# Chunked RWKV-7 in a hybrid trunk: three inverses in turn on half banks, packed squares, sliced products

## The chip, the cores and the metric

One core of a Trainium2 chip runs the whole program in one launch. The metric is device time in microseconds, the median of several executions. TensorE (PE in the views, PEld its weight loads) does matmuls and transposes, VectorE (DVE) and ScalarE (ACT) work on tiles and copy out of PSUM, GpSimd (POOL) does some products in SBUF, and SyncE (SP) issues most DMAs.

## The reference

One inference step of a decoder trunk of two layers, all in float32: 512 prompt tokens behind 16 meta tokens, and 8 sample rows of one token each, which share the weights. The kernel keeps all of them as T = 536 columns (528 of the prompt, TP, and 8 of the samples).

```
for each layer:
  x += 1/2 SwiGLU_a(RMSNorm(x));  x += Mixer(RMSNorm(x));  x += 1/2 SwiGLU_b(RMSNorm(x))
even mixer: HGRN2 (4 heads of 128) beside RWKV-7 (8 heads of 64), one output projection
odd mixer:  GLA (4 heads, keys 128, values 256)
RWKV-7, per head and token:
  S_t = S_{t-1} diag(w_t) + (S_{t-1} (-kk_t)) (kk_t * a_t)^T + v_t k_t^T;   y_t = S_t r_t
HGRN2, GLA: S_t = diag(f_t) S_{t-1} + k_t v_t^T;   o_t = S_t^T q_t
RWKV-7 output: group norm of y per head, plus a bonus term, times a gate; HGRN2 output: RMSNorm
```

The states of the samples come in as inputs and leave as outputs; the prompt starts from zero.

## The kernel before, in words

Activations are held with channels on the 128 partitions and tokens along the free axis. Each large projection is a run of **dense** matmuls (L240 to L242 and L334 to L336): operands are split into a high and a low part (`hh`, `hl`, `whi`, `wlo`) and three products are summed in a PSUM bank of tag `d`.

**RWKV-7 on the prompt** is computed in chunks (`CHUNKS`, one of 16 tokens and eight of 64), for two head pairs at a time: group d = 0 or 1 holds the pairs 2d and 2d+1, so there are 18 chunk problems. `waves(pool, R)` (L1121) writes them as steps. `stage_g` lays four rows of a chunk (keys, values and the two of the update) out in the block tile `bd` (row layout, L1155), multiplies them against each other (L1159 to L1161) and transposes them (L1170). Then the inverse of a triangular matrix is built by doubling: `lev_t` (product L1182, from level 2 a transpose L1187, copies by ScalarE L1188 and L1190) and `lev_x` (L1204, a masked copy by VectorE L1206), over five levels (three for the chunk of 16). When an inverse is done, five steps use it: `st_p` (L1215 to L1224), `st_t`, `st_sa` (L1236), `st_s` (state, L1251) and `st_y` (L1261, L1264). A table `slots` sets the order of all 280 steps: the two groups run side by side, the second `LAG` places behind, and the five output steps of a chunk stand among the next chunk's levels, a place each.

**PSUM.** There are eight banks of 2 KB per partition. `psum(d=2, m=2, w=4)` gives the waves two banks for dense work, two for the HGRN2 core and the sample rows (`m`) and four for `waves` (`w`); `bank(tag)` hands out the next one of a tag's ring.

**The order on TensorE** is written by hand in `even_mixer` (the block under `tc.manual_schedule`): its instructions are issued there in the order in which the generators emit them. The loop takes one step of `waves`, then fills. Every `SAMPLE_EVERY`-th step it takes one piece of `ts`, the sample rows of RWKV-7 (`rsample`, L1060, four pairs one after the other: transposes, a round through DRAM, then products on GpSimd and sums on VectorE, with the tiles `acc` and `sq` that exist once each). Every `POST_EVERY`-th step it takes a piece of `po`, the group norm and gate (`rpost`, L1304) of one span of tokens out of `SPANS`; `post()` starts only when the HGRN2 projections of the fourth head exist (`3 not in H`), and `hgrn_norm` comes before it once the HGRN2 cores are done. `hgrn_norm` sums squares in `acc` and `sq`, and `rpost` uses the same two tiles. After each step the loop adds `FILL` to a credit (in columns of dense work) and spends it on `th_`: the projections and cores of HGRN2 (`hproj`, `hcore`), then the first half of the output projection (`mix_out`). What is left of `th_`, `po` and `mo` follows after the last step. The HGRN2 core of one head (`gla_core`) goes over eight levels of scores (L627, L638 on TensorE; decayed keys L658 on GpSimd); `gla_step` beside it does the sample rows, with the output product of the states at L736. The odd mixer uses the same two functions.

```
credit = min(credit + FILL, FILL_MAX)
while credit > 0:
    cost = next(th_, None)
```

Outside the even mixer (FFNs, odd mixer) nothing of this order is touched, save the output product of `gla_step`.

## Time and profile before

| What | Value |
|---|---|
| Runs, us | 2305.34, 2306.35, 2305.53 (median 2305.53) |
| The execution profiled, us | 2313.27 (span 2311.5) |
| TensorE busy | 2256.8 us, 98% |
| Its weight loads | 2206.5 us, 95% |
| VectorE busy | 1646.7 us, 71% |
| ScalarE busy | 1082.8 us, 47% |
| GpSimd busy | 143.5 us, 6% |
| TensorE clock granted, mean | 0.991 |

The even mixer's waves take from about 516 us to 868 us of the span. A float32 matmul of the non-dense kind has two records in the trace, so that a group with x280 is 140 matmuls. The share of busy time is an average over stages with different limits; what a change is worth in a stage is read from the waits and durations there. Of TensorE's clock the column PEclk gives the part of full speed that was granted: 1.00 is 2.4 GHz, 0.50 is 1.2 GHz.

### The profile page before, as it was taken

Reading aid. Unit: us, or ns where it says so; the run is one execution under the profiler, and the core shown is the slowest. Engines: PE = TensorE matmul, PEld = TensorE weight load, DVE = VectorE, ACT = ScalarE, POOL = GpSimd, SP = SyncE. Lnnn points to the kernel's source line nnn. Section 1 sums busy time; section 2 is a strip of 40 time slices with the busy share of each in tenths; the row PEclk is TensorE's granted clock in tenths of the full one; section 3 lists DMA queues with packets and bytes.
Section 4 is the critical chain, followed back from the end, with each engine's and each line's share of the span. In section 5 each row is a group of like instructions: output and inputs, shape, how many; then the busy total and the mean of one; then the engine's idle time right before and its main releaser. Section 6 shows DMA issues by size and latency. Waiting matters only on the chain.

```text
span 2311.5 us, 47443 instructions
## 1 busy us (share of the span) xinstructions
PE 2256.8 (98%) x19520; PEld 2206.5 (95%) x19520; DVE 1646.7 (71%) x2971; ACT 1082.8 (47%) x2056; POOL 143.5 (6%) x192
## 2 busy tenths in 40 slices
PE   8999999999999999999999999999999999999998
PEld 8999999998998888999999999999999889999998
DVE  7858576686666878966757885857666777948576
ACT  6525254374444456434535452525434464525355
POOL 0000000312212100000000000000021210000000
PEclk9999999999999999999999999999999999999999
DMA  6323334223222116242423332333434353333324
GB/s 171 106 78 101 92 92 132 81 64 94 79 71 72 49 49 167 74 119 75 118 74 101 92 110 74 101 92 94 128 110 128 111 160 92 92 92 101 110 85 136
DMA packets 409393, 229.23 MB, mean 99 GB/s; under 512 B 19252, under 2 KB 400501, under 8 KB 409176
## 3 DMA queue, kind: packets, MB, share of 16 engines
q1 hardware_dynamic: 408456, 224.78, 33.5%
q8 instruction: 153, 2.51, 0.5%
q10 hardware_dynamic: 720, 1.42, 0.2%
q14 instruction: 64, 0.52, 0.1%
HBM read 211.19 MB, written 14.97 MB: 98 GB/s over the span
## 4 chain that ended last, share of the span: by engine, by line
PE 86%; DVE 5%; DMA 3%; ACT 2%; issue 1%; POOL 1%; SPq 0%; ACTq 0%; POOLq 0%; DVEq 0%
PE d L334 21%; PE d L335 21%; PE d L336 21%; PE d L240 5%; PE d L242 4%; PE d L241 4%; PE w L1182 1%; PE w L1204 1%; DMA vb<-dv 1%; DVE wlo L229 1%; DMA raw<-in_even_w_out_dram 1%; PE m L155 1%; DMA sq<-dr 1%; DMA raw<-in_odd_w_out_dram 1%; PE w L1187 1%
## 5 line engine op out<-in xcount | busy, mean ns | idle before, releaser
L240 PE MATMUL d<-hh,whi 128*128 128x264 f32 (+2 forms) x1136 | 343.6, 303 | 2.0 <-DVE xT L596 1.3
L242 PE MATMUL d<-hh,wlo 128*128 128x264 f32 (+2 forms) x1136 | 326.7, 288 | 1.9 <-DVE wlo L229 1.7
L241 PE MATMUL d<-hl,whi 128*128 128x264 f32 (+2 forms) x1136 | 326.6, 288 | 0.5 <-DVE hl L1418 0.5
L334 PE MATMUL d<-hh,whi 128*128 128x268 f32 (+1 forms) x832 | 237.8, 286 | 1.8 <-ACT hh L187 1.3
L335 PE MATMUL d<-hl,whi 128*128 128x268 f32 (+1 forms) x832 | 238.1, 286 | 0.9 <-DVE hl L188 0.9
L336 PE MATMUL d<-hh,wlo 128*128 128x268 f32 (+1 forms) x832 | 237.7, 286 | 0.7 <-DVE wlo L293 0.7
L240 PEld LDWEIGHTS d<-hh,whi 128*128 128x128 f32 x1136 | 216.1, 190 | 7.5 <-issue 2.4
L242 PEld LDWEIGHTS d<-hh,wlo 128*128 128x128 f32 x1136 | 215.4, 190 | 4.6 <-DVE wlo L229 4.0
L241 PEld LDWEIGHTS d<-hl,whi 128*128 128x128 f32 x1136 | 216.3, 190 | 0.9 <-DVE hl L1418 0.7
L534 DVE SCALAR_TENSOR_TENSOR xT<-d,xT 128x272 f32<-128x272 f32 (+2 forms) x192 | 82.9, 433 | 166.7 <-PE d L336 166.6
L334 PE MATMUL d<-hid,whi 128*128 128x264 f32 (+2 forms) x704 | 201.5, 287 | 0.0
L334 PE MATMUL d<-hid,whix 128*128 128x264 f32 (+2 forms) x704 | 201.2, 286 | 0.0
L335 PE MATMUL d<-hid,whix 128*128 128x264 f32 (+2 forms) x704 | 200.8, 285 | 0.0
L335 PE MATMUL d<-hid,whi 128*128 128x264 f32 (+2 forms) x704 | 200.7, 286 | 0.0
L336 PE MATMUL d<-hid,wlox 128*128 128x264 f32 (+2 forms) x704 | 200.6, 285 | 0.0
L336 PE MATMUL d<-hid,wlo 128*128 128x264 f32 (+2 forms) x704 | 200.5, 286 | 0.0
L334 PE MATMUL d<-sumh,whix 128*128 128x268 f32 (+1 forms) x576 | 170.9, 297 | 0.0
L336 PE MATMUL d<-sumh,wlo 128*128 128x268 f32 (+1 forms) x576 | 164.7, 286 | 0.0
L335 PE MATMUL d<-suml,whix 128*128 128x268 f32 (+1 forms) x576 | 164.4, 285 | 0.0
L334 PE MATMUL d<-sumh,whi 128*128 128x268 f32 (+1 forms) x576 | 164.2, 285 | 0.0
L336 PE MATMUL d<-sumh,wlox 128*128 128x268 f32 (+1 forms) x576 | 164.0, 285 | 0.0
L335 PE MATMUL d<-suml,whi 128*128 128x268 f32 (+1 forms) x576 | 164.0, 285 | 0.0
(383 smaller groups left out, 6557.8 us busy)
## 6 DMA issues: line engine op xcount, KB each, us to landing
raw<-in_ffn_gate_dram SPq DMA_DIRECT2D x44, 512.0 KB
raw<-in_ffn_up_dram SPq DMA_DIRECT2D x44, 512.0 KB
rawx<-in_ffn_gate_dram SPq DMA_DIRECT2D x44, 512.0 KB
rawx<-in_ffn_up_dram SPq DMA_DIRECT2D x44, 512.0 KB
raw<-in_ffn_down_dram SPq DMA_DIRECT2D x32, 512.0 KB
rawx<-in_ffn_down_dram SPq DMA_DIRECT2D x32, 512.0 KB
raw<-in_even_w_in_dram SPq DMA_DIRECT2D x30, 512.0 KB
raw<-in_odd_w_in_dram SPq DMA_DIRECT2D x25, 512.0 KB
```

Source lines behind the costliest of these rows:

```text
L155: nc.tensor.matmul(ps[:, :b - a], lhsT, rhs[:, a:b], start=True, stop=True)
L229: nc.vector.tensor_sub(lo[:, ks], raw[:, ks], hi[:, ks].bitcast(F32))
L240: nc.tensor.matmul(o, hi[:, k], h, start=(k == 0), stop=False)
L241: nc.tensor.matmul(o, hi[:, k], l, start=False, stop=False)
L242: nc.tensor.matmul(o, lo[:, k], h, start=False, stop=(k == nk - 1))
L334: nc.tensor.matmul(o, hi[:, k], rh(k), start=start and k == 0, stop=False, **kw)
L335: nc.tensor.matmul(o, hi[:, k], rl(k), start=False, stop=False, **kw)
L336: nc.tensor.matmul(o, lo[:, k], rh(k), start=False, stop=stop and k == nk - 1, **kw)
L534: nc.vector.scalar_tensor_tensor(xv[:, sl], ps, -0.5, xv[:, sl], ALU.mult, ALU.add)
L1182: nc.tensor.matmul(pt[rs, 128 * i:128 * i + cs.stop], U["gm"][ks, i, rs], U["xx"][ks, i, cs], start=True, stop=True)
L1187: nc.tensor.transpose(px[:, 128 * i:128 * i + 128], U["xx"][:, i, 0:128], ident)
L1204: nc.tensor.matmul(pd[:, i], lhsT, rhs, start=True, stop=True)
```

## The change

It changes the order of the waves and the size of several of their products:

- **Three inverses side by side** (`CHAINS`) instead of two. The 18 chunk problems alternate between the groups and take the next free of three chains; a chain's steps stand `CHAINS` places apart, the chains start `STAGGER` apart, and the five output steps stand `OUT_STEP` places apart.
- **Half banks.** `bank("w")` hands out the two halves of one bank one after the other; the first stage takes two halves for its products, and one product of level 0 for both pairs shares a half.
- **Packed squares.** The products L1182 and L1204 of all levels but the last keep only the 32-column blocks on the diagonal: four matmuls with 32 columns of the left operand in the place of one with 128 (`squares_mm`); the result of a pair is 32 columns wide, and `into` spreads it under the mask. The level-0 product is cut in the same way.
- **Row layout copies** (`bd`) are made by ScalarE instead of VectorE.
- **Slices.** The output product of the sample states in `gla_step` is cut into four slices of 32 columns, that of `st_y` into two of 64.
- **Fill.** `FILL` is 550 instead of 1100, `SAMPLE_EVERY` 6 instead of 3, `POST_EVERY` 5 instead of 3, and the first span of `SPANS` is cut in two.

The diff, cut to its core:

```diff
-FILL, FILL_MAX = 1100, 5000
+FILL, FILL_MAX = 550, 5000
...
-SAMPLE_EVERY, POST_EVERY = 3, 3
-SPANS = [0, 272, 400, 536]
-LAG, LAG_LATER = 2, 3
+SAMPLE_EVERY, POST_EVERY = 6, 5
+SPANS = [0, 144, 272, 400, 536]
+CHAINS, STAGGER, OUT_STEP = 3, 4, 2
...
     def bank(tag="m"):
-        return til(rings[tag][0], [P, 512], tag)
+        if tag != "w":
+            return til(rings[tag][0], [P, 512], tag)
+        if not halves:
+            t = til(rings[tag][0], [P, 512], tag)
+            halves.extend((t[:, 256:512], t[:, 0:256]))
+        return halves.pop()
...
-                    nc.tensor.matmul(po[:, c:c + 1], st[:, b, 128 * i:128 * i + 128],
-                                     q[:, TP + b0 + b:TP + b0 + b + 1], start=True, stop=True)
+                    for r in range(0, P, 32):
+                        nc.tensor.matmul(po[r:r + 32, c:c + 1], st[:, b, 128 * i + r:128 * i + r + 32],
+                                         q[:, TP + b0 + b:TP + b0 + b + 1], start=True, stop=True)
...
-                    nc.vector.tensor_copy(dst, Q["sl"][hs, 0:4, t0:t0 + n].rearrange("p v (a l) -> p v a l", l=nl))
-                g = bank("w")
+                    nc.scalar.copy(dst, Q["sl"][hs, 0:4, t0:t0 + n].rearrange("p v (a l) -> p v a l", l=nl))
+                g, gl = bank("w"), bank("w")
...
-                nc.tensor.matmul(g[:, 0:128], b_[:, 384:512], b_[:, 0:128], start=True, stop=True)
+                lt = gl if i == 0 else lt
+                for a in range(na):
+                    for h in range(2):
+                        q = 64 * a + 32 * h
+                        nc.tensor.matmul(lt[q:q + 32, 32 * i:32 * i + nl], b_[:, 384 + q:416 + q],
+                                         Q["sl"][:, 0, t0 + 32 * a:t0 + 32 * a + nl], start=True, stop=True)
...
-                nc.vector.copy_predicated(U["xx"][:, i, 0:128], cu[:, CU_R:CU_R + 128], g[:, 0:128])
...
+                nc.tensor.transpose(gl[:, 128:256], b_[:, 0:128], ident)
                 pt = bank("w")
-                for v in range(3):
-                    nc.tensor.transpose(pt[:, 128 * v:128 * v + 128], b_[:, 128 * v:128 * v + 128], ident)
-                nc.scalar.copy(U["tm"][:, i], pt[:, :384])
+                for v in range(2):
+                    nc.tensor.transpose(pt[:, 128 * v:128 * v + 128], b_[:, 128 * v + 128:128 * v + 256], ident)
+                nc.scalar.copy(U["tm"][:, i, 0:128], gl[:, 128:256])
+                nc.scalar.copy(U["tm"][:, i, 128:384], pt)
+            into(U, 0, lt, 64 * na, nl)
...
+        def into(U, li, ps, rows, nl):
+            src = ps[:rows, 0:64].rearrange("p (u c) -> p u c", u=2)[:, :, :nl]
+            mk = cu[:rows, CU_R + 256 * li:CU_R + 256 * li + 128].rearrange("p (b c) -> p b c", b=4)
+            xx = U["xx"][:rows, :, 0:128].rearrange("p u (b c) -> p u b c", b=4)
+            nc.vector.copy_predicated(xx[:, :, :, :nl], mk.unsqueeze(1).to_broadcast([rows, 2, 4, 32])[:, :, :, :nl],
+                                      src.unsqueeze(2).to_broadcast([rows, 2, 4, nl]))
+        def squares_mm(ps, lhs, rhs):
+            for i in range(2):
+                for q in range(0, P, 32):
+                    nc.tensor.matmul(ps[q:q + 32, 32 * i:32 * i + 32], lhs[:, i, q:q + 32], rhs(i, q),
+                                     start=True, stop=True)
...
+            else:
+                U["t1"] = til(pool, [P, 2, 32], "t1c", bufs=CHAINS)
+                squares_mm(pt, U["gm"], lambda i, q: U["xx"][:, i, q:q + 32])
...
+            if not last:
+                squares_mm(ps, xx[:, :, 128:256], lambda i, q: t1[:, i])
+                into(U, li, ps, P, 32)
+                return
...
-                nc.tensor.matmul(py[:, 64 * i:64 * i + n], U["sa"][:, i], U["gm"][:, i, 128:128 + n],
-                                 start=True, stop=True)
+                for r in (slice(0, 64), slice(64, 128)):
+                    nc.tensor.matmul(py[r, 64 * i:64 * i + n], U["sa"][:, i, r], U["gm"][:, i, 128:128 + n],
+                                     start=True, stop=True)
...
+        free = [STAGGER * i for i in range(CHAINS)]
+        after, ends = [0, 0], []
+        for c in range(18):
+            d, w, U = c % 2, c // 2, {}
+            k = free.index(min(free))
+            t = max(free[k], ends[c - CHAINS - 1] if c > CHAINS else 0)
+            for fn in inverse(d, w, U):
+                slots.setdefault(t, []).append((1 + k, fn, 0))
+                t += CHAINS
+            free[k] = t
+            t = max(t - CHAINS + 2, after[d])
+            for i, st in enumerate((st_p, st_t, st_sa, st_s, st_y)):
+                fn = lambda st=st, d=d, w=w, U=U: st(d, w, U)
+                slots.setdefault(t + OUT_STEP * i, []).append((0, fn, int(i == 4)))
+            after[d] = t + 4 * OUT_STEP
+            ends.append(after[d])
```

In the order of the whole program TensorE's instructions go from 17633 to 18889: the 136 matmuls each of L1182 and L1204 that are not of the last level become 544 each with 32 columns, the 36 of L1159 become 136, and the 96 of L736 become 384. The 280 steps of the waves stay 280. Between the first and the last inverse there are 351 dense matmuls where there were 579.

How the order moves is shown at three places. First TensorE in a first stage, before (`bd` is the row layout of a pair, `sl` the rows themselves, `cf` the identity; the number behind `w` is the PSUM tile's):

```order
L1159 MATMUL w_9717<-bd_820_6034 128x128
L1160 MATMUL w_9717<-sl_613_4515,bd_820_6034 128x128
L1161 MATMUL w_9717<-sl_613_4515,bd_820_6034 128x128
L1170 MATMUL w_9724<-cf_66,bd_820_6034 128x128 x3
L1159 MATMUL w_9731<-bd_821_6036 128x128
L1160 MATMUL w_9731<-sl_616_4518,bd_821_6036 128x128
L1161 MATMUL w_9731<-sl_616_4518,bd_821_6036 128x128
L1170 MATMUL w_9738<-cf_66,bd_821_6036 128x128 x3
```

Here products and transposes take tiles w_9717, w_9724, w_9731 and w_9738, a bank each. Now, with the semaphores that an instruction waits on (DVE, Activation and PE stand for VectorE, ScalarE and TensorE itself):

```order
L1175 MATMUL w_8114<-sl_607_4509,bd_820_6034 32x32 [waits PE_49]
L1175 MATMUL w_8114<-sl_607_4509,bd_820_6034 32x32 x3
L1177 MATMUL w_8114<-sl_607_4509,bd_820_6034 128x128
L1178 MATMUL w_8114<-sl_607_4509,bd_820_6034 128x128
L1184 MATMUL w_8114<-cf_66,bd_820_6034 128x128 [waits DVE_49]
L1187 MATMUL w_8124<-cf_66,bd_820_6034 128x128 [waits PE_49]
L1187 MATMUL w_8124<-cf_66,bd_820_6034 128x128
L1175 MATMUL w_8114<-sl_610_4512,bd_821_6036 32x32 [waits Activation_49]
L1175 MATMUL w_8114<-sl_610_4512,bd_821_6036 32x32 x3
L1177 MATMUL w_8124<-sl_610_4512,bd_821_6036 128x128 [waits Activation_49]
L1178 MATMUL w_8124<-sl_610_4512,bd_821_6036 128x128
```

The transpose of the first pair goes into w_8114, the tile of its products, and waits for VectorE; the second pair's products go into w_8114 and w_8124, which the first pair used, and wait for ScalarE.

Second, TensorE around the transposes of the fourth pair's sample rows (L1069 before, L1081 now), before (`d` is dense work, `hh` and `hl` its left, `whi` and `wlo` its right operands):

```order
L1236 MATMUL w_8471<-pp_8419,xx_7878 128x128 x2
L240 MATMUL d_8318<-hh_70,whi_8311 128x272
L241 MATMUL d_8318<-hl_71,whi_8311 128x272
L242 MATMUL d_8318<-hh_70,wlo_8312 128x272
L1204 MATMUL w_8479<-t_1333_8425,xx_8375 128x128 x2
L1069 MATMUL m_8484<-cf_66,sl_616_4518 8x128
L1069 MATMUL m_8484<-cf_66,ws_618_4520 8x128
L1069 MATMUL m_8484<-cf_66,sl_616_4518 8x128 x2
L1069 MATMUL m_8493<-cf_66,sl_616_4518 8x128
L240 MATMUL d_8318<-hh_70,whi_8311 128x272
```

They stand among the levels of the inverses, with dense matmuls before and behind. Now (L723 and L724 are the outputs of the fourth HGRN2 core; L166 into `m` is the sum of squares of `hgrn_norm` from `acc`, L166 into `w` the group norm of `rpost`):

```order
L723 MATMUL m_11098<-acc_10813,vt_11065 128x128
L724 MATMUL m_11098<-hq_10197,S_11090 128x128
L1081 MATMUL m_11115<-cf_66,sl_616_4518 8x128
L1081 MATMUL m_11115<-cf_66,ws_618_4520 8x128
L1081 MATMUL m_11115<-cf_66,sl_616_4518 8x128 x2
L1081 MATMUL m_11124<-cf_66,sl_616_4518 8x128
L166 MATMUL m_11169<-acc_11157,cf_66 128x272
L166 MATMUL m_11173<-acc_11157,cf_66 128x264
L166 MATMUL w_11190<-sl_607_4509,cf_66 128x144
L166 MATMUL w_11190<-sl_610_4512,cf_66 128x144
L166 MATMUL w_11197<-acc_11189,cf_66 128x144
```

They stand behind the last wave and behind the fourth head's core, and the sum of `hgrn_norm` and the group norm of the first span follow with nothing between.

Third, GpSimd at the same place, before (L1091 to L1115 are the products of the sample rows, L658 the decayed keys of an HGRN2 core):

```order
L658 TENSOR_TENSOR hk_7598<-hk_7598,dlev_8267 128x16x16
L1091 TENSOR_TENSOR sq_8566<-acc_8564,sq_8566 128x512
L658 TENSOR_TENSOR hk_7598<-hk_7598,dlev_8267 128x8x32
L1098 TENSOR_TENSOR acc_8564<-acc_8564,sq_8738 128x512
L658 TENSOR_TENSOR hk_7598<-hk_7598,dlev_8267 128x4x64
L1102 TENSOR_TENSOR sq_8832<-sq_8832,ws_618_4520 128x512
L1103 TENSOR_TENSOR acc_8564<-acc_8564,sq_8832 128x512
L1108 TENSOR_TENSOR sq_8905<-sq_8905,sl_616_4518 128x512
L1109 TENSOR_TENSOR acc_8564<-acc_8564,sq_8905 128x512
L1115 TENSOR_TENSOR sq_9040<-acc_8564,sq_9040 128x512
```

The sample products of the last pair run among the key products of the third head. Now (L669 are the key products, L1103 to L1127 the sample products):

```order
L669 TENSOR_TENSOR hk_10558<-hk_10558,dlev_10816 128x16x16
L669 TENSOR_TENSOR hk_10558<-hk_10558,dlev_10816 128x8x32
L669 TENSOR_TENSOR hk_10558<-hk_10558,dlev_10816 128x4x64
L1103 TENSOR_TENSOR sq_11132<-acc_11130,sq_11132 128x512
L1110 TENSOR_TENSOR acc_11130<-acc_11130,sq_11137 128x512
L1114 TENSOR_TENSOR sq_11141<-sq_11141,ws_618_4520 128x512
L1115 TENSOR_TENSOR acc_11130<-acc_11130,sq_11141 128x512
L1120 TENSOR_TENSOR sq_11146<-sq_11146,sl_616_4518 128x512
L1121 TENSOR_TENSOR acc_11130<-acc_11130,sq_11146 128x512
L1127 TENSOR_TENSOR sq_11152<-acc_11130,sq_11152 128x512
```

They come behind the last key product of the fourth head, with nothing of the even mixer behind them.

## Rows read from the trace of the kernel before

**Rows 1.** The page, busy time of each engine (us, share of the span, records).

```profile
PE 2256.8 (98%) x19520; PEld 2206.5 (95%) x19520; DVE 1646.7 (71%) x2971; ACT 1082.8 (47%) x2056; POOL 143.5 (6%) x192
```

**Rows 2.** Windows: length, busy us and records of PE, PEld, DVE, ACT, POOL; PEclk, DMA share, GB/s.

```profile
516.00:868.00 352.00, 332.73 (x3439) 311.02 (x3437) 247.34 (x713) 163.29 (x441) 71.45 (x78) 0.98 0.24 69
```

**Rows 3.** Groups by line and form on PE: busy us, mean ns of one record.

```profile
L1182 PE MATMUL w<-xx,gm 128*128 128x128 f32 x280 | 45.0, 284 | 1.9 <-DVE xx L1206 1.9
L1204 PE MATMUL w<-t,xx 128*128 128x128 f32 x272 | 43.2, 283 | 1.3 <-ACT xx L1190 0.6 <-ACT t L1188 0.5
L736 PE MATMUL m<-hq,st 128*128 128x1 f32 x192 | 25.9, 239 | 2.1 <-DVE acc L621 1.2 <-ACT whi L228 0.8
```

**Rows 4.** Timeline of one level step in the waves: start us, us, engine, line, operation.

```profile
776.49 0.61 PE L1182 MATMUL w<-xx,gm 128*128 128x128 f32 x4
776.93 0.38 PE L1187 MATMUL w<-cf,xx 128*128 128x128 f32 x2
777.18 0.37 ACT L1188 COPY t<-w 128x256 f32<-128x256 f32 x1 [0.44 <-PE w L1182]
777.45 0.38 ACT L1190 COPY xx<-w 128x256 f32<-128x256 f32 x1
```

**Rows 5.** Timeline of PE in the odd mixer, runs of 32-column operands and one-column products.

```profile
1692.52 0.46 PE L627 MATMUL m<-hq,hk 128*32 128x32 f32 x32
1692.90 0.39 PE L240 MATMUL d<-hh,whi 128*128 128x256 f32 x1
1693.13 0.28 PE L241 MATMUL d<-hl,whi 128*128 128x256 f32 x1
...
1850.92 0.50 PE L736 MATMUL m<-hq,st 128*128 128x1 f32 x4
1851.36 0.46 PE L627 MATMUL m<-hq,hk 128*32 128x32 f32 x32
```

**Rows 6.** Timeline of a first stage in the waves.

```profile
820.59 0.49 PE L1170 MATMUL w<-cf,bd 128*128 128x128 f32 x3
...
821.12 0.48 ACT L1171 COPY tm<-w 128x384 f32<-128x384 f32 x1
...
821.19 0.35 DVE L1166 TENSOR_TENSOR gm<-w,cf 128x192 f32<-128x192 f32 x1
```

**Rows 7.** The same timeline, two copies out of one bank by two engines.

```profile
820.12 0.26 ACT L1222 COPY pd<-w 64x128 f32<-64x128 f32 x1
...
820.41 0.29 DVE L1222 COPY pd<-w 64x128 f32<-64x128 f32 x1 [1.00 <-ACT pd L1222]
```

**Rows 8.** Timeline of one pair's sample step: its first transpose, last product, last sum.

```profile
642.85 0.27 PE L1069 MATMUL m<-cf,sl 128*8 128x128 f32 x1
...
680.57 1.29 POOL L1115 TENSOR_TENSOR sq<-acc,sq 128x512 f32<-128x512 f32 x1 [4.22 <-DMA sq<-dr]
...
682.04 0.69 DVE L1117 TENSOR_REDUCE sl<-sq 128x8 f32<-128x512 f32 x1
```

**Rows 9.** Timeline of GpSimd, key product of one level of an HGRN2 core.

```profile
791.80 0.92 POOL L658 TENSOR_TENSOR hk<-hk,dlev 128x264 f32<-128x264 f32 x1
```

**Rows 10.** Timeline of PE and of DVE, one round of the group norm; HGRN2 norm.

```profile
817.07 0.71 PE L155 MATMUL w<-sl,cf 128*128 128x128 f32 x4
...
822.89 0.95 DVE L1319 RECIPROCAL sl<-sl 128x128 f32<-128x128 f32 x1
...
829.35 0.28 DVE L1328 TENSOR_TENSOR hl<-sq,hh 128x128 fp32r<-128x128 f32 x1
...
837.10 3.51 DVE L166 RECIPROCAL rstd<-rstd 128x272 f32<-128x272 f32 x2
...
846.74 0.77 DVE L869 SCALAR_TENSOR_TENSOR hl<-oa,vcol,hh 128x536 fp32r<-128x536 f32 x1
```

**Rows 11.** Windows of PE behind the HGRN2 norm: length, busy us and records, PEclk, DMA share, GB/s.

```profile
844.00:847.00 3.00, 1.84 (x9) 0.57 0.00 0
847.00:850.00 3.00, 3.00 (x14) 0.50 0.00 0
```

More of the change, by code (lines that the diff above doesn't have):

```diff
@@ L126, in psum @@
             return
+        halves.clear()
         banks.close()
@@ L1171, in stage_g @@
-                nc.scalar.copy(U["tm"][:, i], pt[:, :384])
-            nc.vector.copy_predicated(U["xx"][:, :, 128:256], lmask(0)[:, :, 128:256], U["gm"][:, :, 0:128])
-        def lev_t(U, li):
-            pt = bank("w")
-            U["t1"] = til(pool, [P, 2, P], "t1", bufs=2)
-            rs, cs = (slice(64, 128), slice(0, 64)) if li == 5 else (slice(0, 128), slice(0, 128))
-            ks = cs
-            for i in range(2):
-                nc.tensor.matmul(pt[rs, 128 * i:128 * i + cs.stop], U["gm"][ks, i, rs], U["xx"][ks, i, cs],
-                                 start=True, stop=True)
+                for v in range(2):
+                    nc.tensor.transpose(pt[:, 128 * v:128 * v + 128], b_[:, 128 * v + 128:128 * v + 256], ident)
@@ new lines, in squares_mm, with lev_t @@
+        def squares_mm(ps, lhs, rhs):
[3 more added lines that the diff above has]
+                                     start=True, stop=True)
+        def lev_t(U, li, last):
+            pt = bank("w")
+            if last:
+                U["t1"] = til(pool, [P, 2, P], "t1", bufs=2)
+                rs, cs = (slice(64, 128), slice(0, 64)) if li == 5 else (slice(0, 128), slice(0, 128))
+                ks = cs
+                for i in range(2):
+                    nc.tensor.matmul(pt[rs, 128 * i:128 * i + cs.stop], U["gm"][ks, i, rs], U["xx"][ks, i, cs],
+                                     start=True, stop=True)
+            else:
+                U["t1"] = til(pool, [P, 2, 32], "t1c", bufs=CHAINS)
+                squares_mm(pt, U["gm"], lambda i, q: U["xx"][:, i, q:q + 32])
@@ L1187, in lev_t @@
                     nc.tensor.transpose(px[:, 128 * i:128 * i + 128], U["xx"][:, i, 0:128], ident)
-            nc.scalar.copy(U["t1"][rs, :, cs], pt[rs, 0:256].rearrange("p (u c) -> p u c", u=2)[:, :, cs])
+            if last:
+                nc.scalar.copy(U["t1"][rs, :, cs], pt[rs, 0:256].rearrange("p (u c) -> p u c", u=2)[:, :, cs])
+            else:
+                nc.scalar.copy(U["t1"], pt[:, 0:64].rearrange("p (u c) -> p u c", u=2))
             if li > 1:
@@ L1192, in lev_x @@
         def lev_x(U, li, last):
-            pd = bank("w")[:, 0:256].rearrange("p (u c) -> p u c", u=2)
+            ps = bank("w")
+            pd = ps[:, 0:256].rearrange("p (u c) -> p u c", u=2)
             xx, t1 = U["xx"], U["t1"]
@@ L1200, in lev_x @@
                 return
+            if not last:
+                squares_mm(ps, xx[:, :, 128:256], lambda i, q: t1[:, i])
+                into(U, li, ps, P, 32)
+                return
             for i in range(2):
-                xt = xx[:, i, 128:256]
-                lhsT, rhs = (t1[:, i], xt) if last else (xt, t1[:, i])
-                nc.tensor.matmul(pd[:, i], lhsT, rhs, start=True, stop=True)
-            sl = slice(128, 256) if last else slice(0, 128)
-            nc.vector.copy_predicated(xx[:, :, sl], lmask(li)[:, :, sl], pd)
+                nc.tensor.matmul(pd[:, i], t1[:, i], xx[:, i, 128:256], start=True, stop=True)
+            nc.vector.copy_predicated(xx[:, :, 128:256], lmask(li)[:, :, 128:256], pd)
         def st_p(d, ci, U):
@@ L1271, in inverse @@
             for li in range(1, nl):
-                yield lambda li=li: lev_t(U, li)
+                yield lambda li=li: lev_t(U, li, li == nl - 1)
                 yield lambda li=li: lev_x(U, li, li == nl - 1)
         slots = {}
-        for d in range(2):
-            t = LAG * d
-            for w in range(9):
-                U = {}
-                for fn in inverse(d, w, U):
-                    slots.setdefault(t, []).append((1 + d, fn, 0))
-                    t += 1
-                if w == 0 and d == 1:
-                    t += LAG_LATER
-                for i, st in enumerate((st_p, st_t, st_sa, st_s, st_y)):
-                    fn = lambda st=st, d=d, w=w, U=U: st(d, w, U)
-                    slots.setdefault(t + i, []).append((0, fn, int(i == 4)))
+        free = [STAGGER * i for i in range(CHAINS)]
[14 more added lines that the diff above has]
+            ends.append(after[d])
         ends = 0
```

21 lines of the change are left out of this document (11 added, 10 removed).

## The prediction

> **What bounds the kernel now.** I read the page first, then the windows of the even mixer, the groups by line, and then the timeline piece by piece. The page says that TensorE is busy for 98% of the span [rows 1]. So the first question for any stretch is what TensorE does there and what it waits for. The edit lies in the even mixer, between about 516 us (first inverse) and 891 us (last group norm); only the slices of the state outputs also reach the odd mixer. In the window of the inverses TensorE is busy 332.7 of 352 us, VectorE 247, ScalarE 163 [rows 2]: 19 us without a matmul, and two engines with room. The inverses are chains of small steps (matmul, copy out of PSUM, matmul), and what hides their copies are the dense matmuls and the other pair's steps put between them on TensorE, whose order is fixed by hand. So two things count: how much TensorE work goes, and whether what stands between dependent steps still covers the copies. The order of the changed program tells the second; the prices are rows.
>
> **1. TensorE work that goes: -50 us.** Two full 128x128 products take 0.44 us, from the start of L1182 at 776.49 to the next start at 776.93 [rows 4]. Thirty-two records with 32-column left operands (sixteen matmuls, two records each) take 0.38 us, from 1692.52 to 1692.90 [rows 5]: 12 ns a record. A pair of products cut into eight slices has sixteen records, 0.19 us, and saves 0.25. L1182 has 280 records and L1204 272 [rows 3], 140 and 136 matmuls; 136 of each become slices, 136 pairs: 34 us. L736 has 192 records, 96 matmuls, at 0.44 us for two [rows 3, 5]; sliced like the squares, 48 pairs give 12 us, 8 of them in the odd mixer. The level-0 product L1159, 36 matmuls of the same shape, becomes four slices each: 36 x 0.125 = 4.5. The output product in halves I count at nothing: its cover is TensorE's own queue, and it could cost or give 2. If every run of eight slices paid a changeover as the first dense matmul behind one does (its record is 0.39 us, the next one's 0.28 [rows 5]), 184 x 0.11 = 20 would be lost: ends -30 and -50. I take -50, since the row's 0.38 already holds its own edges.
>
> The Trainium skill says otherwise for slices: "TensorEngine Tiling (Array Packing)", Performance Considerations, under Instruction Overhead, gives each matmul about 60 cycles however few columns it streams, and warns against tiling along a dimension that is already small. By it sixteen records of 25 ns (an estimate from that page, at 2.4 GHz) would cost 0.40 us, the term would shrink to about -7, and the sum would be 43 us higher. The rows disagree, 12 ns a record for 32 columns; I go by the rows.
>
> **2. Two tiles in one bank: +63 us.** This is what the change takes away without saying so. The half that is written second belongs to the same tile as the first, and the program orders accesses to a bank even where they touch other parts: two copies of different halves of the partitions, by ScalarE and VectorE, run one behind the other, VectorE waiting for ScalarE's [rows 7]. So TensorE cannot write the second half while the first is still being copied out. In the order of the change TensorE's rows at the second half carry such a wait where no operand comes from the engine waited for. Before, each of these tiles had a bank of its own, and four took turns.
> Inside the first stage: the transposes at 820.59 come straight behind the products; VectorE's last read of the product bank ends at 821.54 [rows 6]. One read of 0.2 us goes, so TensorE would wait about 0.8 us there, 18 times: 14 us. The second pair's products then wait for ScalarE's copies of the first's transposes (a copy that ends at 821.60, 1.0 us behind their issue [rows 6], with 0.3 to 0.5 us of TensorE work between): 0.5 x 18 = 9.
> Between steps: a copy for ScalarE starts 0.69 us behind the issue of its products, and 0.25 us behind TensorE's last free slot, and lasts 0.37; a second one follows 0.27 later [rows 4]. From TensorE's free slot to the end of the copies it is 0.6 us for one and 0.9 for two; slices end sooner, and I take 0.6. Of the successions of two steps in one bank the order of the change has 67 with nothing in between, 51 with three to six dense matmuls (0.4 us or more), 13 with other products. 67 x 0.6 = 40; the covered ones I count at nothing, at most 51 x 0.6 = 31. Ends: 23 (inside the first stage alone) and 94; 63 is taken, as nothing else stands between those 67.
> ScalarE's new copies of the row layout (72, some 0.3 us each as VectorE's were) lie beside: 163 us of 352 busy [rows 2]. VectorE's gain costs and gives nothing for the same reason.
>
> **3. Work that loses its cover: +78 us.** FILL is halved while the number of steps stays at 280, so of the dense matmuls in the inverses' stretch 351 are left where 579 stood; the rest comes behind. The fourth head's projection ends only there, its core runs behind that with no dense matmul beside it, and everything in post() waits for it. Three bare pieces follow each other on TensorE:
> The last core: a level is a group of scores (0.46 us [rows 5]), then the key product on GpSimd (0.92 [rows 9]) and two hand-overs: 1.5 us, of which TensorE works 0.5. Eight levels, 8 us of waiting; transposes, state chain and state loads some 5 more: +13 (ends 6 and 20).
> The last pair's sample step: taken every sixth step, three of the four pairs are through at the end of the waves. On TensorE the transposes of the fourth now stand ahead of hgrn_norm's sum, whose "acc" tile is free only when the sample step is over; nothing lies between. One such chain ran from 642.85 to 682.73 [rows 8]: 40 us. The squares and sums behind (seven operations of 0.77, by the row of that size at 846.74 [rows 10]) are 5 more; TensorE's own part is 0.5: +44. Low end: seven GpSimd steps of 1.29 and five transfers at the 4.22 waited for the last [rows 8], 30. High end: eight reloads of the residual (2.1 MB) stand in the same SP queue; at the rate that the window's 69 GB/s with a DMA share of 0.24 makes in full [rows 2], 7 us: 52.
> Group norm of two spans, bare: norm 10.4 us of VectorE from 837.10 to 847.5, then four rounds. One round of 128 columns took 12.6 us among other work (817.07 to 829.63); alone it has two reciprocals of 0.95 and some fourteen operations of 0.28, 5.8, and about 1.4 for TensorE and ScalarE between them [rows 10]: 7.2. 10.4 + 4 x 7.2 = 39, of which TensorE works 8 (34 products at 0.22 or a little more, as in [rows 4]): +31 (ends 20 and 50).
> Of the 19 us that TensorE waited in this stretch [rows 2], about half belonged to these pieces and goes with them: -10.
>
> **4. Clock: +9 us.** Behind a lull at 841 to 846 us the granted clock stood at 0.57 and 0.50 for six us, the lower level [rows 11]. Three such lulls are new; each returns at 1.2 GHz for about six us, 3 us lost: +9 (0 to 30).
>
> **Sum.** -50 + 63 + 78 + 9 = +100. The execution profiled took 2313.27 us, its span 2311.5; with the sum 2413. The median shown is 7.7 lower, so 2305.5 + 100 = 2405 us. With the ends of each part together: -50 + 23 + 46 + 0 = +19 and -30 + 94 + 112 + 30 = +206, both too far for all at once.
>
> **Rivals.**
> A. Only the bare pieces count. The steps of one inverse stand three places apart instead of one, so waits at half banks may fall where a step would have waited for its own data anyway. For it: two engines with room [rows 2]. Against: the 67 bare successions. 2405 - 63 = 2342 us.
> B. The clock falls in the waves as well. If a third of the 230 us or so of TensorE work there ran at 0.50, as at 844 to 850 [rows 11], it would be 75 us more: 2480. Against: the new waits are each under 1 us. The Trainium skill, "TensorE: Matmul & The Clock Gate", under HAM oscillation, tells of kernels whose short waits between bursts bring the low clock back each time; no row here has such a pattern for long.
> C. Faster: ScalarE, VectorE and GpSimd run so far ahead of TensorE that its order hardly waits, at half banks or behind the waves. The place is the stretch from 516 us on, the price the 50 us of work less what waits remain; it decides as soon as the new waits stay under 50 us of the 150 counted. With 20 left, 2305 - 50 + 20 = 2275 us. For it: VectorE at 70% and ScalarE at 46% of the window [rows 2]. Against: the sample chain, 40 us by itself, starts from a TensorE transpose.
> D. The change doesn't do what it says, the three chains being serial through their banks: that is part 2, and in the forecast.
>
> **How the numbers follow.** Forecast 0.50 (its own range 2355 to 2460), A 0.20, B 0.12, slower in some other way 0.04, C 0.11, and 0.03 for within 0.2% (4.6 us, about what a measurement of this kernel can tell from no change). Faster 0.11, same 0.03, slower 0.86. From 2330 to 2480 the forecast, A and half of B lie inside; C, no change and the rest of B are left out.
>
> **What would show it.** L1205 at about 12 ns a record confirms part 1. Waits of TensorE on ScalarE and VectorE summing to 60 us or more between first and last inverse confirm part 2; under 25, A holds. A stretch of some 40 us with hardly a matmul, ended by the squares of hgrn_norm, confirms the sample step; a TensorE that is busy there refutes part 3. Low clock only behind lulls confirms part 4, all over the waves B. Wrong altogether if the last dense matmul of the even mixer comes earlier than before.

## The result, and the profile after

The changed kernel takes 2524.93 us (median of 4 runs, 2515.43 to 2535.08) where the kernel before takes 2305.94 (2305.34 to 2310.21): a ratio of 1.0946, 95% interval 1.0901 to 1.0991, slower by 219 us. The execution profiled took 2535.08 us, its span is 2533.3. The forecast was slower by 100, and 2480 its upper end.

Three lines of the page after: the span, the busy time of the engines (before it is [rows 1]) and the granted clock in forty slices of the span, in tenths:

```profile
span 2533.3 us, 52525 instructions
...
PE 2329.4 (92%) x22032; PEld 2215.2 (87%) x22032; DVE 1638.3 (65%) x2917; ACT 1111.9 (44%) x2176; POOL 139.9 (6%) x192
...
PEclk9999999977968885599999999999999999999999
```

TensorE is busy for longer, not shorter, and still its share falls from 98% to 92%. The clock row says why both can be: in eight of the nine slices from about 510 to 1080 us its digit is below 9, where before none was.

Where the loss lies, the windows tell. The first matmul of the FFN behind the even mixer starts at 918.1 us before and at 1142.2 after, both from a first product of the waves at 520 us; behind it the two kernels take 1393.4 and 1391.1 us. So all of the loss, 224 us between the two profiled executions, lies in this stretch, which I count from 516 us as in [rows 2]. I cut it where the waves end (their last transposes of states), at 868 and 912 us. Windows of before, the second half of the stretch (the first half is [rows 2]):

```profile
868.00:918.00 50.00, 46.87 (x366) 45.07 (x364) 38.88 (x87) 28.62 (x63) 0.00 (x0) 1.00 0.64 176
```

The same two halves after:

```profile
516.00:912.00 396.00, 319.67 (x4640) 253.36 (x4638) 156.83 (x447) 156.97 (x478) 46.40 (x54) 0.80 0.14 40
912.00:1142.00 230.00, 138.31 (x1291) 122.23 (x1290) 126.05 (x308) 67.94 (x153) 20.81 (x24) 0.75 0.27 78
```

TensorE is idle for 76 us in the waves and 92 behind them (before: 19 and 3). The granted clock is 0.80 and 0.75 (before: 0.98 and 1.00). The windows of after that lie wholly at the lower level (four of them here, and the sums over all, for the waves and for what follows):

```profile
720.97:744.86 23.89, 21.66 (x311) 0.50 0.06 18
...
809.71:840.43 30.72, 26.47 (x239) 0.50 0.22 61
...
sum 156.91, PE 133.97; mean PE 12.18
```

```profile
987.21:1028.17 40.96, 3.90 (x10) 0.50 0.30 96
1031.58:1069.13 37.55, 22.23 (x77) 0.50 0.00 0
...
sum 116.16, PE 50.59; mean PE 8.43
```

So 157 us of the waves and 116 us behind them ran at 1.2 GHz, and TensorE worked in 134 and 51 of these. If work at half the clock takes twice as long, 67 and 25 us are lost. That is an estimate; in the kernel before, a dense matmul starts 0.23 us behind the one ahead at a clock of 0.50 (about 850 us) and 0.13 us behind it at 1.00 (about 852 us), which is a little less than twice.

What TensorE waited for in the waves of after (line, releaser, us in all, times, longest):

```profile
PE w L1184 <- DVE gm L1182: 12.6, 18, 1.7
PE w L1205 <- ACT py L1267: 8.2, 9, 1.7
PE w L1175 <- ACT tm L1189: 5.7, 9, 0.6
PE w L1205 <- ACT xx L1231: 4.8, 12, 0.7
PE w L1279 <- ACT xx L1231: 3.1, 7, 0.5
```

The first and the third are the two waits of the first stage at half banks, 18 and 9 times. The rest are level products and output steps behind the copy of the step ahead. No single wait in these waves is longer than 2.0 us. In the waves of before the largest line is

```profile
PE w L1182 <- DVE xx L1206: 2.3, 4, 0.9
```

### The profile page after: what moved, and what is told of

It is laid out like the page before. It is cut to its first block, busy times and chain, and to the rows that moved or that the text cites. A ratio compares the mean times of both kernels' runs of the same rounds, so it can differ in the third digit from the quotient of the medians.

```text
span 2533.3 us, 52525 instructions
## 1 busy us (share of the span) xinstructions
PE 2329.4 (92%) x22032; PEld 2215.2 (87%) x22032; DVE 1638.3 (65%) x2917; ACT 1111.9 (44%) x2176; POOL 139.9 (6%) x192
## 5 line engine op out<-in xcount | busy, mean ns | idle before, releaser
L251 PE MATMUL d<-hh,whi 128*128 128x264 f32 (+2 forms) x1136 | 351.2, 310 | 4.6 <-ACT whi L239 2.4
L253 PE MATMUL d<-hh,wlo 128*128 128x264 f32 (+2 forms) x1136 | 332.7, 294 | 2.0 <-DVE wlo L240 1.9
L252 PE MATMUL d<-hl,whi 128*128 128x264 f32 (+2 forms) x1136 | 333.3, 294 | 0.0
L251 PEld LDWEIGHTS d<-hh,whi 128*128 128x128 f32 x1136 | 221.5, 195 | 12.7 <-ACT whi L239 3.7
L253 PEld LDWEIGHTS d<-hh,wlo 128*128 128x128 f32 x1136 | 222.0, 196 | 4.6 <-DVE wlo L240 3.9
L252 PEld LDWEIGHTS d<-hl,whi 128*128 128x128 f32 x1136 | 222.7, 196 | 0.7 <-issue 0.3
```

The source lines that it names most:

```text
L251: nc.tensor.matmul(o, hi[:, k], h, start=(k == 0), stop=False)
L252: nc.tensor.matmul(o, hi[:, k], l, start=False, stop=False)
L253: nc.tensor.matmul(o, lo[:, k], h, start=False, stop=(k == nk - 1))
```

## The experiments

Each run's stretch is cut, as above, at the end of its waves and at the next FFN; the rows are windows with the columns of [rows 2].

**1. A bank for each tile.** The changed kernel with `bank("w")` handing out whole banks; the first stage needs one for its products and one for its transposes.

```diff
-        if not halves:
-            t = til(rings[tag][0], [P, 512], tag)
-            halves.extend((t[:, 256:512], t[:, 0:256]))
-        return halves.pop()
+        return til(rings[tag][0], [P, 512], tag)
...
-                g, gl = bank("w"), bank("w")
+                g = bank("w")
...
-                lt = gl if i == 0 else lt
+                lt = g[:, 256:320]
```

> The changed kernel, but every tile of tag w has a bank of its own again (a first stage takes one bank for its products and one for its three transposes, as before the change); all else stays: three chains, slices, thin fill. Theory (half banks): in the changed kernel TensorE stands idle for 76 of the 390 us from 516 us to the end of the waves, and 147 us there are at the low clock; with own banks the idle time falls to 20 to 35 us, the low clock follows it to under 60 us, and the time falls by 70 to 100 us, to about 2440. Rival 1 (thin fill): with half the dense matmuls between the steps each step waits for its own copies whatever its bank; idle time stays over 60 us and the time within 20 us of the changed kernel's 2525. Rival 2 (the 32-column slices themselves bring the low clock): idle time falls, the low clock stays over 110 us, time about 2475. In all three the stretch behind the waves stays as it is (236 us up to the next FFN).

Measured: 2386.49 us (2 runs, 2380.29 and 2392.69), 139 less than the changed kernel. (The 147 us in the expectation was read with an offset; by the windows above it is 157.) Its two halves:

```profile
516.00:777.00 261.00, 248.98 (x4638) 207.38 (x4637) 150.77 (x464) 149.36 (x442) 47.21 (x54) 1.00 0.22 60
777.00:985.00 208.00, 130.01 (x1295) 118.93 (x1294) 121.52 (x303) 65.85 (x151) 20.21 (x24) 0.77 0.30 86
```

The waves shrink from 396 to 261 us. 64 of the 135 us are idle time (76 to 12); the other 71 are almost the same records (4638 for 4640), which take 249.0 us at a clock of 1.00 where they took 319.7 at 0.80. Both rivals fall: the fill was as thin as in the changed kernel and the slices were all there. The theory's 70 to 100 us were too few, as it did not expect the low clock to vanish altogether. It also missed the stretch behind the waves, which it took as unchanged and which is 22 us shorter (230 to 208). TensorE waits 14 us less there (92 to 78): the group norm's products use the same banks, and their waits sum to 27 us in the changed kernel and to 14 here.

**2. The fill back, half banks kept.**

```diff
-FILL, FILL_MAX = 550, 5000
+FILL, FILL_MAX = 1100, 5000
-SAMPLE_EVERY, POST_EVERY = 6, 5
+SAMPLE_EVERY, POST_EVERY = 3, 3
```

> The changed kernel with FILL 1100, SAMPLE_EVERY 3 and POST_EVERY 3, as before the change; half banks, chains and slices stay. Theory (half banks in the waves, lost cover behind them): the pieces behind the waves (92 us of idle TensorE and some 125 us at the low clock) mostly go, 110 to 140 us; in the waves a part of the waits at half banks stays, at least 35 us of idle time, with low clock in places: about 2390 to 2410. Rival 1 (thin fill is behind the waits in the waves too): the idle time of the waves falls to about 20 us and the clock is back at 1.00 nearly throughout: 2280 or lower, faster than before the change. Rival 2 (slices bring the low clock): 2380 with over 100 us at the low clock in the waves although TensorE is idle for less than 30 us.

The execution profiled took 2449.01 us; the only other one took 4358.71, which nothing else in the study resembles, and is left out. The halves:

```profile
516.00:980.00 464.00, 377.09 (x5509) 303.56 (x5507) 225.31 (x629) 186.38 (x552) 68.64 (x78) 0.83 0.19 52
980.00:1056.00 76.00, 59.26 (x419) 54.38 (x419) 53.85 (x126) 35.89 (x79) 0.00 (x0) 0.93 0.46 127
```

What stood behind the waves is hidden (230 to 76 us), as the theory had it. But in the waves TensorE is idle for 87 us, no less than with the thin fill, and the clock is 0.83. Rival 1 falls with that, and my "at least 35" was far too low. The dense matmuls cover a wait only where they stand. Counted in TensorE's timeline (waits of over 0.15 us), 67 of the 87 us are 104 waits straight behind another product of the waves, and 9 are 14 waits behind three or more dense matmuls. In the changed kernel it is 65 us in 104 waits and 4 us in 12. So the dense matmuls that came back did not make the bare places fewer.

**3. Both.** The edits of 1 and 2 together.

> The changed kernel with both: a bank for each tile of tag w, and FILL 1100, SAMPLE_EVERY 3, POST_EVERY 3. What is left of the change is three chains, slices, packed squares and the row layout copies on ScalarE. Theory (half banks and lost cover are the whole loss): 2260 to 2290, the 45 us of TensorE work gained less a few us of waits, clock as before the change. Rival (three chains side by side wait for each other's banks and copies, or slices lower the clock): 2320 or more, with over 40 us of idle TensorE or over 60 us at the low clock in the waves.

Measured: 2321.98 us, ratio 1.007 (1.0049 to 1.0091). Its waves:

```profile
516.00:857.00 341.00, 314.77 (x5518) 266.01 (x5516) 222.83 (x646) 179.44 (x513) 69.20 (x78) 0.97 0.24 70
```

Neither side holds. The time is in the rival's range, but TensorE is idle for 26 us and at the low clock for 20, far less than the rival asks; almost all of the 219 us is back, but the 45 us of gain that the theory added is not there.

**4. The thin fill alone**, on the kernel before.

```diff
-FILL, FILL_MAX = 1100, 5000
+FILL, FILL_MAX = 550, 5000
-SAMPLE_EVERY, POST_EVERY = 3, 3
+SAMPLE_EVERY, POST_EVERY = 6, 5
```

> The kernel before with nothing but FILL 550, SAMPLE_EVERY 6 and POST_EVERY 5; two chains, a bank for each tile, full products. It shows what the fill alone costs. Theory (half banks in the waves): the pieces behind the waves appear as in the changed kernel, 90 us or so of idle time plus the low clock behind it, and in the waves TensorE waits little more than before (19 us then, under 35 now): 2400 to 2430. Rival 1 (thin fill): the waves show the idle time and the low clock of the changed kernel too (over 60 us idle, over 100 us at the low clock): 2480 to 2530.

Measured: 2403.73 us, ratio 1.0425 (1.0344 to 1.0506), and

```profile
516.00:812.00 296.00, 271.49 (x2637) 255.19 (x2636) 175.22 (x532) 132.26 (x369) 47.66 (x54) 0.96 0.19 52
812.00:1020.00 208.00, 131.18 (x1164) 118.06 (x1163) 119.33 (x270) 62.88 (x138) 19.90 (x24) 0.76 0.30 86
```

The theory is confirmed: TensorE is idle for 25 us in the waves, at a clock of 0.96, and nearly the whole loss lies behind them, where 208 us stand for 50 (the waves are 56 us shorter, with fewer dense matmuls in them).

**5. The packed squares alone**, on the kernel before: `squares_mm`, `into` and the two callers of the change, nothing else.

```diff
-            for i in range(2):
-                nc.tensor.matmul(pt[rs, 128 * i:128 * i + cs.stop], U["gm"][ks, i, rs], U["xx"][ks, i, cs],
+                squares_mm(pt, U["gm"], lambda i, q: U["xx"][:, i, q:q + 32])
...
+                squares_mm(ps, xx[:, :, 128:256], lambda i, q: t1[:, i])
+                into(U, li, ps, P, 32)
```

> The kernel before with the packed squares alone: the products of L1182 and L1204 of all levels but the last in slices of 32 columns, their results packed and spread by VectorE; two chains, own banks, fill, state outputs and row layout copies as before. Theory of the prediction (a run of 16 such records takes 0.19 us where two full products take 0.44): 34 us of TensorE work go, 2270 to 2280. Rival (a run costs 0.26 us and another 0.1 at each changeover between narrow and full left operands, as the trace of the changed kernel with own banks has it): what is gained in the run is given back at its edges, 2295 to 2310, within 0.4% of before.

Measured: 2305.16 us, ratio 1.0000 (0.9985 to 1.0015). The time is the rival's. The rows show how a gain can be seen and not reach the time. Groups of before are [rows 3], 45.0 and 43.2 us; those of this run:

```profile
L1186 PE MATMUL w<-xx,gm 128*32 128x32 f32 x1088 | 23.0, 204 | 4.2 <-DVE xx L1179 3.2 <-DVE dlev L660 0.9
L1186 PE MATMUL w<-t1c,xx 128*32 128x32 f32 x1088 | 22.2, 201 | 1.5 <-DVE gm L1166 1.0 <-ACT t1c L1210 0.4
```

By the groups some 42 us of busy time are gone (88 less 45, and 1.3 for the four matmuls of L1182 that stay whole). Between dense matmuls the timeline has nothing gone. Two full products between dense matmuls, in the kernel before:

```profile
586.80 0.29 PE L242 MATMUL d<-hh,wlo 128*128 128x272 f32 x1
586.93 0.61 PE L1204 MATMUL w<-t,xx 128*128 128x128 f32 x4
587.29 0.37 PE L240 MATMUL d<-hh,whi 128*128 128x272 f32 x1
587.50 0.29 PE L241 MATMUL d<-hl,whi 128*128 128x272 f32 x1
```

Eight slices in their place, in the run with own banks:

```profile
560.32 0.28 PE L247 MATMUL d<-hh,wlo 128*128 128x264 f32 x1
560.53 0.33 PE L1199 MATMUL w<-t1c,xx 128*32 128x32 f32 x16
560.79 0.39 PE L245 MATMUL d<-hh,whi 128*128 128x264 f32 x1
561.02 0.28 PE L246 MATMUL d<-hl,whi 128*128 128x264 f32 x1
```

From the last dense start ahead to the second dense start behind it is 0.70 us in both. The run itself is shorter (0.26 for 0.36), but it starts 0.21 us behind the dense matmul's start in the place of 0.13, and the dense one behind it takes 0.23 in the place of 0.21. That is one place, with dense matmuls of 264 columns for 272, but run 5's own timeline says the same: with dense matmuls on both sides the median of 30 places is 0.71 us, and of 31 places before 0.69 (all at the full clock and without a wait). Where a dense matmul is ahead and another product of the waves behind, a little is gained: 0.64 us in 27 places for 0.68 in 35.

So some work does go. The first half of the stretch in run 5 ([rows 2] is before):

```profile
516.00:861.00 345.00, 321.08 (x5056) 278.80 (x5056) 243.53 (x713) 153.50 (x438) 68.83 (x76) 0.97 0.25 71
```

In this execution the whole stretch is 7 us shorter than before, 395 for 402. The ten executions don't show it in their time, but they do in their clock: their mean span is 2304.7 us at a mean granted clock of 0.991, that of nineteen executions of before 2304.8 at 0.994. Span times clock, as an estimate of the time at full clock, is 7 us lower. Some 7 of the 34 us went, then, and the lower clock took them back. Why the clock is lower was not tried.

**6. The sample states' output in slices alone**, the edit of `gla_step` on the kernel before.

```diff
-                    nc.tensor.matmul(po[:, c:c + 1], st[:, b, 128 * i:128 * i + 128],
+                    for r in range(0, P, 32):
+                        nc.tensor.matmul(po[r:r + 32, c:c + 1], st[:, b, 128 * i + r:128 * i + r + 32],
```

> The kernel before with nothing but the output product of gla_step in four slices of 32 columns. Theory of the prediction: 12 us less, about 2292. Rival (the edges of each run of slices give it back): within 4 us of before.

Measured: 2306.25 us, ratio 0.9998 (0.9984 to 1.0012). The rival holds here too. By the estimate of run 5 (0.993 for 0.994) some 2 us of work went.

**7. The sample steps among the waves.** Run 1 with one number changed.

```diff
-SAMPLE_EVERY, POST_EVERY = 6, 5
+SAMPLE_EVERY, POST_EVERY = 3, 5
```

> The changed kernel with a bank for each tile of tag w, as in the run with own banks (2386), and SAMPLE_EVERY 3 in the place of 6; FILL stays at 550, POST_EVERY at 5. The four pairs' sample steps are then all among the waves. Theory (the last pair's sample step stands bare behind the waves, and TensorE waits 40 us for it in one piece): that wait is gone, and with it some of the low clock behind it, 2320 to 2345. Rival (the wait for acc only uncovers another one of the same chain, the group norm or the fourth core, which runs beside it): over 2365.

Measured: 2352.28 us (2 runs), 34 less than run 1: 7 us above the theory's range and 13 under the rival's. The waits of TensorE behind the waves show the mechanism. In run 1, then in this one:

```profile
PE m L160 <- DVE acc L185: 39.6, 1, 39.6
```

```profile
PE m L160 <- DVE acc L185: 2.3, 1, 2.3
PE w L160 <- DVE acc L1363: 6.8, 2, 6.5
```

The wait of 39.6 us is gone, and the stretch behind the waves is 38 us shorter (208 to 170). The waves took 10 us more (261 to 271) with the samples among them. So the theory's mechanism holds, with a part given back that it had not counted: these 10 us, and a wait of the group norm that is 6.8 us where run 1 has 2.6.

**8. Half banks in turn.** The changed kernel; two banks are opened at once and their halves handed out crosswise.

```diff
-            t = til(rings[tag][0], [P, 512], tag)
-            halves.extend((t[:, 256:512], t[:, 0:256]))
+            t, u = (til(rings[tag][0], [P, 512], tag) for _ in range(2))
+            halves.extend((u[:, 256:512], t[:, 256:512], u[:, 0:256], t[:, 0:256]))
```

> The changed kernel, half banks kept, but handed out over two banks in turn (first half of one bank, first half of the next, second half of the first, second half of the next), so that two tiles in succession never share a bank. Theory (the waits in the waves come from the second half of a bank following straight behind the first): most of the 76 us of idle time in the waves goes, 20 to 40 us are left, the low clock falls to under 60 us, and the time is 2410 to 2450. Rival (it is the number of banks' worth of tiles in flight, not their succession): idle time stays over 60 us and the time over 2490.

Measured: 2424.39 us (2 runs), 101 less than the changed kernel.

```profile
516.00:819.00 303.00, 266.53 (x4637) 215.23 (x4637) 152.89 (x446) 156.85 (x478) 47.88 (x54) 0.96 0.19 52
```

Idle time in the waves falls from 76 to 36 us and the clock rises to 0.96, with as many halves and as many banks as in the changed kernel. So most of the 64 us that own banks took away comes from the second half straight behind the first. The largest line that is left is the first stage's transposes:

```profile
PE w L1187 <- DVE gm L1182: 9.4, 15, 1.3
```

Two tiles' distance is not enough there; with own banks, in a ring of four, 12 us of idle time are left.

**9 to 12. What remains when banks and fill are as before.** Run 9 is the kernel before with the row layout copies on ScalarE; run 10 is run 3 with the three spans of before; run 11 is run 3 with two chains (CHAINS 2, STAGGER 5); run 12 is run 5 with the row layout copies on ScalarE.

```diff
-                    nc.vector.tensor_copy(dst, Q["sl"][hs, 0:4, t0:t0 + n].rearrange("p v (a l) -> p v a l", l=nl))
+                    nc.scalar.copy(dst, Q["sl"][hs, 0:4, t0:t0 + n].rearrange("p v (a l) -> p v a l", l=nl))
...
-SPANS = [0, 144, 272, 400, 536]
+SPANS = [0, 272, 400, 536]
...
-CHAINS, STAGGER, OUT_STEP = 3, 4, 2
+CHAINS, STAGGER, OUT_STEP = 2, 5, 2
```

> The kernel before with the row layout copies (bd) on ScalarE in the place of VectorE, and nothing else. Theory (they lie beside TensorE's work on either engine): within 4 us of before. Rival (ScalarE, which also copies every level's product and transpose out, now delays the next first stage): 5 to 15 us slower.

> The run with own banks and the fill of before (2322) with SPANS as before the change, three spans in the place of four. Its stretch behind the waves was 64 us where that of before has 50. Theory (the fourth span's rounds of group norm are the difference): 8 to 14 us less, 2308 to 2314. Rival (three chains leave the last chunks later): no change, 2318 to 2326.

> The run with own banks and the fill of before (2322) with two chains (CHAINS 2, STAGGER 5) in the place of three; four spans, slices and row layout copies on ScalarE stay. Theory (three chains bring nothing once each tile has a bank, as the fill covers the copies of two as well): within 5 us of 2322. Rival 1 (three chains make the output steps wait): 2305 to 2315. Rival 2 (three chains do help): 2330 or more.

> The kernel before with packed squares and the row layout copies on ScalarE: the two parts of the change that take work off VectorE and none that takes cover away, the version most likely to beat both kernels. Theory (neither lies on the path): within 4 us of before. Rival (VectorE's shorter masked copies and lighter queue let TensorE's 19 us of waits in the waves shrink): 2290 to 2300.

Measured: run 9 2307.01 us, ratio 1.0015 (1.0000 to 1.0030), as the theory had it. Run 10 2304.43 us, ratio 0.9994 (0.9981 to 1.0007): 17.5 us less than run 3, more than the 8 to 14 expected, so the fourth span was all that was left of the loss. Run 11 2326.59 us, ratio 1.0098 (1.0070 to 1.0126), within 5 us of run 3: three chains bring nothing that can be measured. Run 12 2308.31 us, ratio 1.0015 (0.9998 to 1.0032): no gain, as the theory had it. No version beat the kernel before by more than can be measured. In runs 10 and 12 the clock has its part in this, as in run 5: their mean granted clocks are 0.990 and 0.989, that of before in the same series is 0.993, and span times clock is 9 and 7 us lower than before.

Read in a row, the runs take the loss apart: changed kernel 2525, own banks 2386 (-139), samples among the waves 2352 (-34), FILL and POST_EVERY as before 2322 (-30), three spans 2304 (-18), where it meets the kernel before. These are differences of medians, of two executions each for the first two runs (run 1's lie 12 us apart). The order matters for the sizes: with half banks still in place the fill alone gave back 76.

## Why the prediction was wrong

The direction and the waits were right; the sum was short by 119 us, because of the clock and of the work. Against the 224 us of the stretch:

- **Waits, parts 2 and 3: right.** The terms 63 and 78 make 141 us; idle time of TensorE in the stretch rose from 22 to 168, by 146. In the waves it is 57 us (76 less 19), and own banks took 64 away. The 18 waits of the first stage, put at 14 us, are 12.6. Behind the waves the wait for `acc`, put at 44 with the sums behind the sample step, is 39.7 in the changed kernel:

```profile
PE m L166 <- DVE acc L191: 39.7, 1, 39.7
```

  Own banks, halves in turn and the thin fill alone (runs 1, 8 and 4) show each mechanism by itself. Part 2 also had the place right: 65 of the 76 us in the waves fall straight behind another product of the waves, and 4 behind dense matmuls. What it left out is that half banks cost the group norm behind the waves 14 us as well (run 1).
- **Part 4, the clock: the step that failed.** It was put at +9 us from three lulls; by the estimate above it is 67 + 25, less some 7 of before (0.98 over 352 us [rows 2]): +85. Run 1 bears out the waves' part, with 71 us in almost the same records. The waves' part was in rival B, with 75 us and a chance of 0.12. Own banks show the mechanism: without the waits the clock in the waves is 1.00. The argument against B, that each new wait is under 1 us, was the mistake: some are up to 2.0 us, and it priced waits one by one, where a stretch of them shares one clock. Behind the waves it is the long lulls, as forecast, but the clock does not come back after six us: in the window from 1031.6 to 1069.1 us, most of it group norm, it is low for 37.6 us, with TensorE busy for 22 of them.
- **Part 1, TensorE work that goes: the other step that failed.** It was put at -50 us (ends -30 and -50); in time runs 5 and 6 measure 0, with 95% intervals of about 3.5 us either way, and some 7 and 2 us of work that the clock took back. The failed reading is the 0.19 us for a run of 16 records, half of a run of 32 in [rows 5]: the run takes 0.26 us, starts 0.09 us later behind a dense matmul than full products do, and the dense matmul behind it takes 0.02 more. The row's 0.38 did not hold its own edges, as the prediction assumed, and halving a run does not halve them. The full pair's 0.44 was also taken next to another full product [rows 4]; between dense matmuls it is 0.36.
- **The rest.** The fourth span costs 18 us by run 10, with banks and fill as before, and no term had named it; what it costs in the changed kernel itself was not tried. ScalarE's row layout copies cost nothing, as forecast (run 9). Rival A falls: the waits at half banks are real and the largest single loss. Rival C falls with them.

Together: 146 of waits and 85 of clock, and -7 of work as what is then left of TensorE's 78 us more of busy time, make the 224. B's own sum, 2480, with the 43 us of part 1 put back that did not come is 2523. That it comes so near to 2525 is in part luck: B had 75 us for the waves, where it is 67, and 9 for what follows them, where it is 25.

On slices the Trainium skill, "TensorEngine Tiling (Array Packing)", under Instruction Overhead, came nearer in its result than my reading of the rows: with its overhead for each of the sixteen records the whole term was about -7 (an estimate from its figure), and runs 5 and 6 have some 7 and 2 us less work. This is in part luck, since that estimate makes the run 0.40 us long and the trace has 0.26. Under Key Properties the same page of the Trainium skill also states that changing the tiling mode drains TensorE. The later start of a run of slices behind a dense matmul, by 0.09 us, would fit a drain; no run here shows that it is one.

On the clock the Trainium skill, "TensorE: Matmul & The Clock Gate", under A second HAM failure mode, tells of a kernel that cycles through PSUM banks and whose frequent short idle gaps between groups of matmuls make the clock go to and fro between its two levels. The waves of the changed kernel fit that, with 0.80 granted and no wait longer than 2.0 us.

## What to carry to other kernels

Two tiles in one PSUM bank, used one straight behind the other, put the copy of the first in front of the matmul of the second; hand out halves of different banks in turn at the least, whole banks at best. When a change adds many short waits to TensorE, price the clock of the whole stretch as well: here 64 us of waits cost 71 us more in almost the same matmuls. Read the clock beside the time also where a change takes work away: in run 5 some 7 us of work went and the time stayed. And a matmul cut into slices is to be priced between the neighbours that it will have, from the last start ahead to the second start behind, not by its group's busy time.

## What was not expected of the hardware

- The lower clock came in the changed kernel's waves although no wait there is longer than 2.0 us. Idle time of TensorE in the waves and their clock: 12 of 261 us and 1.00 (run 1), 19 of 352 and 0.98 (before), 25 of 296 and 0.96 (run 4), 36 of 303 and 0.96 (run 8), 87 of 464 and 0.83 (run 2), 76 of 396 and 0.80 (changed kernel). Which of the waits brought it down in each place was not tried apart.
- Sixteen records with 32-column left operands take 0.26 us as a run, and between dense matmuls they are, with their edges, as long as the four records with 128 columns that they replace: 0.71 us against 0.69 in the median.
- Whether two halves of a bank could be written and read at once, if the program did not order them, was not tried: every version here orders them.
